# adaLN's later vectors in a pool of their own, half of them beside V, and S1 of h inside the retention

## The chip, the cores and the metric

The kernel runs on one core of a Trainium2 chip. The metric is the time of one execution in microseconds of the device. Before the change it is 1793.54 us, the median of three runs (1792.5 to 1797.46).

## The reference, cut to what matters

One decoder layer on x of 1024 tokens by 1024 channels, all float32. The vector c gives six vectors of 1024 by one matrix, `w_ada`:

```python
mod = jnp.dot(jax.nn.silu(c), w_ada) + b_ada
shift1, scale1, gate1, shift2, scale2, gate2 = split(mod, 6)
h = _rmsnorm(x, norm1_w) * (1.0 + scale1) + shift1
proj = jnp.dot(h, w_in)      # q, k, v of attention, the indexer's iq, ik, iw, retention's q, k, v and gate, two gates
att = _dsa_attention(...)    # each query keeps the 256 keys with the highest indexer score
ret = _retention(...)        # chunks of 128 tokens, four heads, a state carried from chunk to chunk
y_r = jnp.dot(silu(gr) * _head_groupnorm(ret, gn_w), w_ret_proj)
merged = sigmoid(ga) * (att @ w_attn_proj) + sigmoid(gb) * y_r
x = x + gate1 * (merged @ w_out)
h2 = _rmsnorm(x, norm2_w) * (1.0 + scale2) + shift2
x = x + gate2 * ((silu(h2 @ w_ffn_gate) * (h2 @ w_ffn_up)) @ w_ffn_down)
out = _rmsnorm(x, final_norm_w)
```

Only shift1 and scale1 are needed to form h. gate1 is needed at the output projection, and shift2, scale2 and gate2 later still.

## The kernel before, in words

**Arithmetic.** A float32 product is made of three matmuls on rounded parts: each operand is kept as hi (rounded) and lo (the rest), and hi*hi, hi*lo and lo*hi are added up in PSUM. ScalarE (ACT) makes hi by a copy, and GpSimd (POOL) or VectorE (DVE) makes lo by a subtraction. A full block is 128 by 512.

**Stages, in order of the code.** (1) The start: x is normalised, shift1 and scale1 are summed on DVE from `w_ada` (`wa`, `acc`, lines 275 to 294), h^T is made (`hT_hi`, `hT_lo`), and six blocks of the gate projection's first half are multiplied. (2) The indexer's projections. (3) V of attention, with the indexer's scores between its matmuls (lines 491 to 507; `units` and `turns_after` fix how they alternate). (4) Retention, two heads at a time: `for hp in range(2)` from line 606. Each pass has a loop over eight token tiles that makes q and k and rotates them on POOL (lines 610 to 634), and one over the chunks (lines 679 to 692). (5) Six blocks of the gate projection's second half (lines 899 to 905). (6) The other projections, each by seven products of half-sized blocks (M1 to M7, Strassen's scheme, lines 712 to 815, 880 to 992). M1, M2 and M4 multiply blocks of h itself; M5, M6, M3 and M7 multiply four combinations of h's blocks, S1, S2, S4 and S3, in that order. (7) The retention's own projection, attention, the output projection, the FFN.

**The four combinations.** Lines 906 to 916: `add_up` adds the parts on DVE into four `sums` tiles, and `split_sum` makes hi on ACT and lo on DVE. S2 goes on from S1's sums and S4 from S2's, in place; S3 is formed anew and lies where a block of h was. S1, S2 and S4 (16 KB of each partition) are in a pool `sp`, which lies at the addresses of the tables and of the retention's pool `retp`, so each tile waits for what it overlaps there.

**adaLN's other vectors.** `mod_work` (lines 518 to 545) is a generator of 32 steps in four groups of eight: for m = 2, 5, 3, 4 (gate1, gate2, shift2, scale2) and eight rows k of 128, it loads 512 KB of `w_ada` (`mw`, three buffers, two loads ahead) and adds them, scaled by silu(c), into `macc` on DVE (lines 536 and 538). There is one `macc`. A group ends with two matmuls and two additions on DVE into PSUM's sums (`mod_gate`), or eight transposes and two reductions (`mod_cols`). One step is called per token tile in both loops of both retention passes.

**What sets the order.** The tile framework plans every engine's order by a simulation: whenever an engine is free it takes, of the instructions that are ready, the one with the lowest priority number, which is the position in the code. An instruction from further down may therefore come early. `tc.cur_priority += LATE` moves a part back by 20000 positions without any wait. On the chip each engine, and the queue of SyncE (SP) that issues all DMAs, keeps the planned order.

**The selection.** `select_all` (line 440) finds the 256th largest score of each row bit by bit: 31 rounds of six counts over the scores (line 454, DVE), at LATE. It fills DVE from the end of the scores on. `turns_after(paused[0], split)` holds the round of bit 8 behind the last split of S3, and line 1028 that of bit 3 behind the last block of the retention's gated output.

Of the kernel before, what the change touches and what calls it, by code (L numbers as in the profile page):

```python
# [8 lines left out]
F32 = mybir.dt.float32  # L9
# [10 lines left out]
P = 128  # L20
# [23 lines left out]
def tile_hybrid_layer(ctx: ExitStack, tc: tile.TileContext, x, c, w_ada, b_ada, norm1_w, w_in,  # L44
# [159 lines left out]
    def ps_mm():  # L204
        return psx.tile([P, H], F32, name="mm", tag="mm", bufs=3)
# [228 lines left out]
    def all_scores():  # L434
        for b in range(2, NT):
            yield from score_units(b)
        select_all()
# [49 lines left out]
        tc.cur_priority -= LATE  # L487

    units = []
    sgen = all_scores()
    slots = [rows_slot([(w_in, C_VA, H)], k) for k in range(KT)]
    for t in range(NT):
        ps = ps_mm()
        for k in range(KT):
            n = 5 * (KT * t + k) // 4 - 8
            while len(units) <= n and next(sgen, LATE) is not LATE:
                pass
            mm = mm_tok(ps, hT.lhs(t), slots, ks=(k,))  # L500
            if n >= 0:
                turns_after(mm, units[min(n, len(units) - 1)])
        st = projp.tile([P, H], F32, name="vst", bufs=2)
        nc.scalar.activation(st, ps, AF.Copy)
        nc.sync.dma_start(out=v_d[:, t], in_=st)
    for _ in sgen:
        pass
    st_i.close()
    st_p.close()
    st_w.close()  # L510


    st_r = ctx.enter_context(ExitStack())
    retp = pool("retp", side="left", stack=st_r)
    ones = retp.tile([P, P], F32, name="ones")
    nc.vector.memset(ones, 1.0)

    def mod_work():

        steps = [(m, k) for m in (2, 5, 3, 4) for k in range(KT)]  # L520
        mw = {}

        def load(n):
            if n < len(steps):
                m, k = steps[n]
                mw[n] = retp.tile([P, D], F32, name="mw", bufs=3)
                nc.sync.dma_start(out=mw[n], in_=w_ada[k * P:(k + 1) * P, m * D:(m + 1) * D])

        load(0)
        load(1)  # L530
        for n, (m, k) in enumerate(steps):
            load(n + 2)
            sc = silu_c[:, k:k + 1]
            if k == 0:
                acc = retp.tile([P, D], F32, name="macc", bufs=1)
# [27 lines left out]
    def mod_gate(m, i, acc):  # L563
        for hf in range(2):
            cs = slice(hf * H, (hf + 1) * H)
            g = retp.tile([P, H], F32, name="gateb", bufs=1)
# [5 lines left out]
            nc.sync.dma_start(out=gate_d[i][:, cs], in_=g)  # L572


    def ret_scale_col(kind, h):
# [10 lines left out]
    def add_up(out, terms):  # L586

        first = True
        for name, k, sign in terms:
            for part in [out] if name is None else [f32(x[:, k, :]) for x in side[name]]:  # L590
# [6 lines left out]
                    nc.vector.tensor_tensor(out, part, acc, op=ALU.subtract)  # L597
                acc, s0 = out, 1

    def split_sum(to, k, src):  # L600
        hi, lo = (x[:, k, :] for x in side[to])
        nc.scalar.activation(hi, src, AF.Copy)
        return nc.vector.tensor_sub(lo, src, f32(hi))

    mgen = mod_work()
    for hp in range(2):
        slots = [rows_slot([(w_in, C_QR + 256 * hp, 256), (w_in, C_KR + 256 * hp, 256)], k) for k in range(KT)]
        qkT = [big_tile(i, [P, 2, 4, P], F32, "qkT") for i in range(4)]
# [1 line left out]
        for t in range(NT):  # L610
            ps = ps_mm()
            mm_tok(ps, hT.lhs(t), slots)
            qk = retp.tile([P, 4, 2, HD], F32, name="qk", bufs=2)
            for i in range(4):
                nc.scalar.activation(qk[:, i], ps[:, i * P:(i + 1) * P].rearrange("p (a b) -> p a b", a=2),  # L615
                                     AF.Copy, scale=ret_scale_col(i // 2, 2 * hp + i % 2))
            ra = big_tile(6, [P, 4, 2, HD], F32, "rra")
            rb = big_tile(7, [P, 4, 2, HD], F32, "rrb")
            rq = retp.tile([P, 2, 2, HD], F32, name="rq", bufs=2)
            cs = cosr[:, t, :].unsqueeze(1).to_broadcast([P, 8, HD])  # L620
            sn = sinr[:, t, :].unsqueeze(1).to_broadcast([P, 4, HD])
# [12 lines left out]
            next(mgen, None)  # L634
        slots = [rows_slot([(w_in, C_VR + 2 * DV * hp, 2 * DV)], k) for k in range(KT)]
        r = [None, None]
        vs, inns = {}, {}
# [41 lines left out]
        for t in range(NT + 1):  # L679
            if t < NT:  # L680
                ps = ps_mm()
                mm_tok(ps, hT.lhs(t), slots)
                vs[t] = retp.tile([P, 2 * DV], F32, name="vs", bufs=3)
                nc.scalar.activation(vs[t], ps, AF.Copy)
                for e in range(2):
                    inner(t, e)
            if t:
                for e in range(2):
                    r[e] = chunk(t - 1, e, r[e])
            next(mgen, None)  # L690
            if t == 0:
                next(mgen, None)
    for _ in mgen:
        pass
    st_r.close()
    st_t.close()

# [195 lines left out]


    kept = [big_tile(4 + i, [P, 2, H], F32, "kept") for i in range(2)]
    sums = [big_tile(6 + i, [P, 2, H], F32, "sums") for i in range(2)]
    sums = [t[:, i, :] for t in sums for i in range(2)]
# [8 lines left out]
    st_s = ctx.enter_context(ExitStack())  # L906
    sp = pool("sp", side="right", stack=st_s)
    for name in ("S1", "S2", "S4"):
        t = sp.tile([P, 2, 4, H], R, name=name, tag=name)
        side[name] = t[:, 0], t[:, 1]  # L910
# [57 lines left out]
    def behind(i):  # L968
        n, m = 2 + (i - 14) // 7, seq[i][1]
        if 14 <= i < n_mid:  # L970
            if m == "M1":
                flow[n + 1].open()
                flow[n].next = flow[n + 1]
            if n in (8, 9) and m == "M1":
                rope[n - 8] = rope_load(n - 8)
            if n in (9, 10) and m == "M5":
                rope_store(n - 9, *rope[n - 9])
        if i == n_mid:
            flow[-1].open()
        k = i - n_mid - 4  # L980
        if k == -1:
            gT.alloc(0)
        if 0 <= k < KT:
            make_g(k, 0, *g_load(k, 0, *(f32(x) for x in ring_pair())))
            if k in (1, 3):
                stage = sp.tile([P, 8, H], F32, name="stage", tag=f"S{(k + 1) // 2}")
# [699 lines left out]
```

## Time and profile before

| | |
|---|---|
| median of three runs | 1793.54 us |
| profiled execution | 1796.41 us, of which the span from first to last instruction is 1794.6 us |
| granted clock of TensorE, mean | 0.987 of full speed |
| TensorE busy | 1703.6 us (95%) |
| DVE busy | 1211.1 us (67%) |
| POOL busy | 891.7 us (50%) |
| DMA | 266.49 MB, 148 GB/s over the span |

PE is TensorE; a row of a timeline gives start, duration, engine, line, operation, what is written from what, its shape, and in brackets the idle time before it with what ended it. PE's ends are modelled, and 512 columns follow each other every 0.23 us although one is shown as 0.39 us. The granted clock is a share of full speed (1.00 is 2.4 GHz).

### The profile page before, as it was taken

The page shows a single profiled execution, that of the slowest core. Times are in us where ns is not written, and L with a number is a line of the kernel's source. Part 1 is how long each engine was busy: PE and PEld are TensorE (multiplying, and loading weights), DVE is VectorE, ACT ScalarE, POOL GpSimd, SP SyncE. Part 2 cuts the span into 40 slices and gives each one's busy share as a digit, 9 for nine tenths or more (in the row PEclk, how much of TensorE's full clock was granted, in tenths as well). Part 3 has the DMA queues.
Part 4 walks back from the last instruction along what each step waited for, and adds up shares of the span by engine and source line. Part 5 has one row for each costly group of instructions (what it writes and reads, how often), then busy time and mean ns, then how long its engine had stood idle before and what let it go on. Part 6 is the DMA issues. An engine that isn't in the chain of part 4 may idle for free. (4 is left out here: it accounts for less than half of the span.)

```text
span 1794.6 us, 24639 instructions
## 1 busy us (share of the span) xinstructions
PE 1703.6 (95%) x8266; PEld 1399.4 (78%) x8266; DVE 1211.1 (67%) x2093; ACT 747.4 (42%) x1466; POOL 891.7 (50%) x883
## 2 busy tenths in 40 slices
PE   5898989999979999999999999999989999999998
PEld 4797867878758888788777888777778887888887
DVE  7627599999699445459876656876665454476565
ACT  3525532431445344430477246733323333354444
POOL 4571284682565489530246640045444444566574
PEclk9999999999989999999999999999999999999999
DMA  8521245243423356775852740266753332387663
GB/s 278 178 74 42 83 123 185 89 138 95 126 80 116 105 152 195 248 212 159 190 128 69 251 162 1 68 232 235 237 190 106 101 111 89 111 274 227 186 181 113
DMA packets 182655, 266.49 MB, mean 148 GB/s; under 512 B 13872, under 2 KB 111616, under 8 KB 180096
## 3 DMA queue, kind: packets, MB, share of 16 engines
q1 hardware_dynamic: 182528, 264.91, 47.4%
q8 instruction: 65, 1.06, 0.3%
q14 instruction: 62, 0.51, 0.1%
HBM read 195.39 MB, written 69.47 MB: 148 GB/s over the span
## 5 line engine op out<-in xcount | busy, mean ns | idle before, releaser
L80 POOL TENSOR_TENSOR wlo<-wraw,whi 128x512 fp32r<-128x512 f32 (+2 forms) x116 | 144.2, 1253 | 103.6 <-ACT whi L77 96.4
L454 DVE TENSOR_SCALAR_CACHE_REDUCE eq<-score,cand 128x384 uint8<-128x384 f32 (+2 forms) x192 | 180.8, 942 | 4.3
L709 POOL TENSOR_TENSOR flo<-tmp,fhi 128x512 fp32r<-128x512 f32 x79 | 105.1, 1331 | 156.8 <-ACT fhi L708 130.5
L120 PE MATMUL mm<-whi,hT_hi 128*128 128x512 f32 (+1 forms) x432 | 163.3, 381 | 2.4 <-ACT qk L615 1.8
L122 PE MATMUL mm<-wlo,hT_hi 128*128 128x512 f32 (+1 forms) x432 | 163.7, 380 | 0.0
L123 PE MATMUL mm<-whi,hT_lo 128*128 128x512 f32 (+1 forms) x432 | 163.4, 379 | 0.0
L785 PE MATMUL ya<-hc,fhi 128*128 128x512 f32 x344 | 136.1, 396 | 12.1 <-DVE c L768 8.6
L1534 DVE TENSOR_TENSOR dslot<-draw,dslot 128x512 fp32r<-128x512 f32 x88 | 90.4, 1053 | 72.4 <-ACT dslot L1533 66.2
L787 PE MATMUL ya<-hc,fhi 128*128 128x512 f32 x344 | 135.0, 392 | 0.0
L789 PE MATMUL ya<-hc,flo 128*128 128x512 f32 x344 | 133.6, 393 | 0.0
L1533 ACT ACTIVATE dslot<-draw 128x512 fp32r<-128x512 f32 x154 | 90.1, 626 | 97.7 <-PE ya L1552 36.6
L1534 POOL TENSOR_TENSOR dslot<-draw,dslot 128x512 fp32r<-128x512 f32 x66 | 96.9, 1478 | 62.7 <-ACT dslot L1533 58.5
L709 POOL TENSOR_TENSOR flo<-raws,fhi 128x512 fp32r<-128x512 f32 x60 | 83.2, 1387 | 87.8 <-ACT fhi L708 62.8
L77 ACT ACTIVATE whi<-wraw 128x512 fp32r<-128x512 f32 (+2 forms) x116 | 66.8, 589 | 123.2 <-DMA wraw<-in_w_in_dram 59.0
L789 PE MATMUL yb<-hc,flo 128*128 128x512 f32 x256 | 100.1, 391 | 4.0 <-POOL flo L709 4.0
L785 PE MATMUL yb<-hc,fhi 128*128 128x512 f32 x256 | 100.4, 392 | 0.2
L787 PE MATMUL yb<-hc,fhi 128*128 128x512 f32 x256 | 99.7, 389 | 0.0
L708 ACT ACTIVATE fhi<-tmp 128x512 fp32r<-128x512 f32 x84 | 53.0, 630 | 111.4 <-PE ya L787 61.2
L709 POOL TENSOR_TENSOR wlo<-wraw,whi 128x512 fp32r<-128x512 f32 x52 | 80.2, 1552 | 30.9 <-ACT whi L708 24.9
L120 PEld LDWEIGHTS mm<-whi,hT_hi 128*128 128x128 f32 x432 | 82.4, 191 | 14.7 <-ACT qk L615 2.2
L1086 POOL TENSOR_SCALAR sx<-sx,mx 128x128 f32<-128x128 f32 (+7 forms) x64 | 47.4, 746 | 92.5 <-DVE mx L1085 69.7
L123 PEld LDWEIGHTS mm<-whi,hT_lo 128*128 128x128 f32 x432 | 82.9, 192 | 13.0
(403 smaller groups left out, 4918.2 us busy)
## 6 DMA issues: line engine op xcount, KB each, us to landing
draw<-act_d SPq DMA_DIRECT2D x77, 256.0 KB
mw<-in_w_ada_dram SPq DMA_DIRECT2D x32, 512.0 KB
act_d<-c SPq DMA_DIRECT2D x64, 256.0 KB
raw<-in_w_in_dram SPq DMA_DIRECT2D x26, 512.0 KB
raws<-in_w_ffn_gate_dram SPq DMA_DIRECT2D x24, 512.0 KB
raws<-in_w_ffn_up_dram SPq DMA_DIRECT2D x24, 512.0 KB
dw<-in_w_ffn_down_dram SPq DMA_DIRECT2D x22, 512.0 KB
dw_d<-dw SPq DMA_DIRECT2D x11, 1024.0 KB
```

Of the source, the lines that this page charges most:

```text
L77: ins = nc.scalar.activation(hi[:, :n], raw[:, :n], AF.Copy)
L80: nc.gpsimd.tensor_sub(lo[:, :n], raw[:, :n], f32(hi[:, :n]))
L120: ins = nc.tensor.matmul(ps, lhsT=ahi, rhs=whi[:, :n], start=(i == 0), stop=False)
L122: nc.tensor.matmul(ps, lhsT=ahi, rhs=wlo[:, :n], start=False, stop=False)
L123: nc.tensor.matmul(ps, lhsT=alo, rhs=whi[:, :n], start=False, stop=(i == last))
L454: ins = [nc.vector.tensor_scalar(eq[:, :sc.shape[1]], sc, thr[j], None, op0=op, op1=ALU.add, accum_out=cnt[:, j:j + 1]) for j, sc in enume ...
L709: (eng or nc.gpsimd).tensor_sub(lo, src, f32(hi))
L785: mm = nc.tensor.matmul(ps, lhsT=whi[:, k, :], rhs=hhi[:, k, :], start=own and k == 0, stop=False, skip_group_check=True)
L787: nc.tensor.matmul(ps, lhsT=whi[:, k, :], rhs=hlo[:, k, :], start=False, stop=False, skip_group_check=True)
L789: nc.tensor.matmul(ps, lhsT=wlo[:, k, :], rhs=hhi[:, k, :], start=False, stop=k == 3, skip_group_check=True)
L1533: nc.scalar.activation(slot[:, 0], raw, AF.Copy)
L1534: lo_eng.tensor_sub(slot[:, 1], raw, f32(slot[:, 0]))
```

## The change

Three edits. First, `mod_work` moves ahead of V's loop with a pool of its own, `modp`, on the right side of SBUF, where nothing lay from the start to the end of the first retention pass; `mw` has two buffers instead of three and one load ahead instead of two. V's loop calls two steps per token tile, at priorities moved back by LATE // 10, which is 2000 positions: 16 calls, the eight steps of m = 2, its end, and seven steps of m = 5. The first retention pass calls the others, and what is left is run out at its end. Second, the second pass calls none; at chunk 2 it allocates the `sums` and S1, which now lies in a pool `sp1` where `modp` was, and at chunks 3 to 6 it forms S1's sums, splits them, and goes on to S2's sums. Third, the stage before M1 only splits S2 and forms S4 and S3 as before, with S2 and S4 in `sp`.

```diff
+    st_m = ctx.enter_context(ExitStack())
+    modp = pool("modp", side="right", stack=st_m)
+    ones = modp.tile([P, P], F32, name="ones")
+    nc.vector.memset(ones, 1.0)
+    def mod_work():
...
-                mw[n] = retp.tile([P, D], F32, name="mw", bufs=3)
+                mw[n] = modp.tile([P, D], F32, name="mw", bufs=2)
...
-        load(0)
-        load(1)
-        for n, (m, k) in enumerate(steps):
-            load(n + 2)
+        load(0)
+        for n, (m, k) in enumerate(steps):
+            load(n + 1)
...
+    def mod_step():
+        tc.cur_priority += LATE // 10
+        next(mgen, None)
+        tc.cur_priority -= LATE // 10
...
                 turns_after(mm, units[min(n, len(units) - 1)])
+        for _ in range(2):
+            mod_step()
         st = projp.tile([P, H], F32, name="vst", bufs=2)
...
+    def alloc_side(pl, name):
+        x = pl.tile([P, 2, 4, H], R, name=name, tag=name)
+        side[name] = x[:, 0], x[:, 1]
...
             nc.scalar.activation(qkT[t // 2][:, t % 2].rearrange("p h t -> p (h t)"), tp, AF.Copy)
-            next(mgen, None)
+            if hp == 0:
+                next(mgen, None)
...
-            next(mgen, None)
-            if t == 0:
-                next(mgen, None)
-    for _ in mgen:
-        pass
+            if hp == 0:
+                next(mgen, None)
+            elif t == 2:
+                sums = [big_tile(6 + i, [P, 2, H], F32, "sums") for i in range(2)]
+                sums = [x[:, i, :] for x in sums for i in range(2)]
+                alloc_side(sp1, "S1")
+            elif 3 <= t < 7:
+                k = t - 3
+                add_up(sums[k], [("h12", k, 1), ("h22", k, 1)])
+                split_sum("S1", k, sums[k])
+                add_up(sums[k], [(None, k, 1), ("h11", k, -1)])
+        if hp == 0:
+            for _ in mgen:
+                pass
+            st_m.close()
+            st_s = ctx.enter_context(ExitStack())
+            sp1 = pool("sp1", side="right", stack=st_s)
...
-    for to, terms in (("S1", [("h12", 1), ("h22", 1)]), ("S2", [(None, 1), ("h11", -1)]),
-                      ("S4", [(None, -1), ("h21", 1)]), ("S3", [("h11", 1), ("h12", -1)])):
+    for to, terms in (("S2", []), ("S4", [(None, -1), ("h21", 1)]), ("S3", [("h11", 1), ("h12", -1)])):
         for k in range(4):
-            add_up(sums[k], [(n, k, sign) for n, sign in terms])
+            if terms:
+                add_up(sums[k], [(n, k, sign) for n, sign in terms])
             split = split_sum(to, k, sums[k])
```

## Rows read from the trace of the kernel before

**Rows 1.** The page's head and its busy time by engine.
```profile
span 1794.6 us, 24639 instructions
PE 1703.6 (95%) x8266; PEld 1399.4 (78%) x8266; DVE 1211.1 (67%) x2093; ACT 747.4 (42%) x1466; POOL 891.7 (50%) x883
```

**Rows 2.** Stretches: length, busy time (count) of PE, PEld, DVE, ACT, POOL; PE's clock, DMA.
```profile
13.00:66.00 53.00, 38.29 (x169) 29.75 (x170) 50.29 (x94) 17.97 (x33) 30.25 (x26) 0.97 0.75 236
66.00:130.00 64.00, 62.95 (x438) 59.56 (x438) 19.94 (x44) 22.20 (x41) 40.16 (x90) 1.00 0.39 110
130.00:230.00 100.00, 94.38 (x451) 78.73 (x449) 65.40 (x106) 56.37 (x112) 23.41 (x25) 0.98 0.21 63
228.00:300.00 72.00, 63.71 (x277) 50.23 (x276) 69.23 (x114) 21.60 (x55) 54.88 (x64) 0.95 0.59 186
495.00:550.00 55.00, 44.14 (x174) 34.53 (x173) 52.55 (x62) 25.06 (x45) 31.50 (x18) 0.91 0.29 86
```

**Rows 3.** PE's order of time: the start of M1, and the first and last wait behind it.
```profile
504.36 0.50 PE L785 MATMUL mm<-hT_hi,whi 128*128 128x512 f32 x1 [0.15 <-ACT spare L904]
515.88 0.50 PE L785 MATMUL mm<-S,whi 128*128 128x512 f32 x1 [3.07 <-ACT kept L765]
533.41 0.80 PE L787 MATMUL lg<-S,whi 128*128 128x512 f32 x1 [1.84 <-DVE S L603]
```

**Rows 4.** Stretches, `sums` alone: busy time of DVE and ACT, then POOL, clock, DMA.
```profile
405.00:430.00 25.00, 7.48 (x12) 0.00 (x0) 0.00 (x0) 1.00 0.13 32
495.00:550.00 55.00, 39.88 (x45) 10.83 (x18) 0.00 (x0) 0.91 0.29 86
```

**Rows 5.** DVE's order of time: splits of the combinations, and the selection's next count.
```profile
497.91 3.48 DVE L603 TENSOR_TENSOR S<-sums,S 128x512 fp32r<-128x512 f32 x2
511.84 0.68 DVE L603 TENSOR_TENSOR S<-sums,S 128x512 fp32r<-128x512 f32 x1
548.63 0.60 DVE L454 TENSOR_SCALAR_CACHE_REDUCE eq<-score,cand 128x384 uint8<-128x384 f32 x1
```

**Rows 6.** A stretch between retention and the combinations.
```profile
480.00:490.00 10.00, 10.00 (x46) 8.28 (x45) 3.39 (x13) 3.10 (x7) 3.59 (x11) 1.00 0.24 81
```

**Rows 7.** `macc`: its additions over the whole span (min/median/max ns, first and last start).
```profile
L538 DVE SCALAR_TENSOR_TENSOR macc<-mw,colT,macc x28: 1268/1318/2166, 236.4 to 447.2; 128x1024 f32<-128x1024 f32 x28
```

**Rows 8.** The first group of steps: DVE, POOL and PE in order of time.
```profile
236.36 1.98 DVE L538 SCALAR_TENSOR_TENSOR macc<-mw,colT,macc 128x1024 f32<-128x1024 f32 x1
239.59 1.43 POOL L627 TENSOR_TENSOR rq<-rra,rrb 128x128 f32<-128x128 f32 x1
259.02 0.47 POOL L627 TENSOR_TENSOR kk<-rra,rrb 128x128 f32<-128x128 f32 x1
241.90 0.33 PE L631 MATMUL tr<-ident,rq 128*128 128x128 f32 x1 [1.73 <-POOL rq L628]
250.55 0.33 PE L632 MATMUL tr<-ident,kk 128*128 128x128 f32 x1 [1.06 <-POOL kk L628]
```

**Rows 9.** The second and third group: PE's waits, and the stretches that hold them.
```profile
294.73 0.49 PE L643 MATMUL tr<-qkT 128*128 128x128 f32 x2 [1.99 <-DVE inn L645]
372.41 0.33 PE L631 MATMUL tr<-ident,rq 128*128 128x128 f32 x1 [2.74 <-POOL rq L628]
250.00:260.00 10.00, 9.45 (x38) 7.67 (x39) 9.75 (x17) 2.33 (x6) 9.84 (x15) 0.83 0.48 153
290.00:300.00 10.00, 8.01 (x31) 6.24 (x30) 9.89 (x22) 0.38 (x1) 0.00 (x0) 0.83 0.95 332
370.00:380.00 10.00, 6.71 (x24) 5.20 (x25) 9.75 (x17) 1.74 (x5) 9.71 (x14) 0.83 0.52 178
```

**Rows 10.** SP: the load of gate1, whose line stands behind attention in the code.
```profile
L1214 SPq DMA_DIRECT2D gate<-gate_d x1: 430/430/430, 291.8 to 291.8; - x1
```

**Rows 11.** DVE in the start: lines of the last tiles of x between `acc`'s.
```profile
50.37 0.75 DVE L235 TENSOR_SCALAR x_t<-x_t,rstd 128x1024 f32<-128x1024 f32 x1
51.38 0.48 DVE L287 SCALAR_TENSOR_TENSOR acc<-wa,colT,acc 128x256 f32<-128x256 f32 x1
```

More of the change, by code (lines that the diff above doesn't have):

```diff
@@ L487, in select_all @@
         tc.cur_priority -= LATE
[L491 to L498, printed above, removed]
-                pass
[L500 to L515, printed above, removed]
+    st_m = ctx.enter_context(ExitStack())
+    modp = pool("modp", side="right", stack=st_m)
+    ones = modp.tile([P, P], F32, name="ones")
     nc.vector.memset(ones, 1.0)
@@ L525, in load @@
                 m, k = steps[n]
-                mw[n] = retp.tile([P, D], F32, name="mw", bufs=3)
+                mw[n] = modp.tile([P, D], F32, name="mw", bufs=2)
                 nc.sync.dma_start(out=mw[n], in_=w_ada[k * P:(k + 1) * P, m * D:(m + 1) * D])
         load(0)
-        load(1)
         for n, (m, k) in enumerate(steps):
-            load(n + 2)
+            load(n + 1)
             sc = silu_c[:, k:k + 1]
             if k == 0:
-                acc = retp.tile([P, D], F32, name="macc", bufs=1)
+                acc = modp.tile([P, D], F32, name="macc", bufs=1)
                 nc.vector.tensor_scalar(acc, mw[n], sc, None, op0=ALU.mult)
@@ L565, in mod_gate @@
             cs = slice(hf * H, (hf + 1) * H)
-            g = retp.tile([P, H], F32, name="gateb", bufs=1)
+            g = modp.tile([P, H], F32, name="gateb", bufs=1)
             nc.sync.dma_start(out=g, in_=b_ada[m * D + hf * H:m * D + (hf + 1) * H]
@@ L572, in mod_gate @@
             nc.sync.dma_start(out=gate_d[i][:, cs], in_=g)
+    mgen = mod_work()
+    def mod_step():
+        tc.cur_priority += LATE // 10
+        next(mgen, None)
+        tc.cur_priority -= LATE // 10
+    units = []
+    sgen = all_scores()
+    slots = [rows_slot([(w_in, C_VA, H)], k) for k in range(KT)]
+    for t in range(NT):
+        ps = ps_mm()
+        for k in range(KT):
+            n = 5 * (KT * t + k) // 4 - 8
+            while len(units) <= n and next(sgen, LATE) is not LATE:
+                pass
+            mm = mm_tok(ps, hT.lhs(t), slots, ks=(k,))
+            if n >= 0:
+                turns_after(mm, units[min(n, len(units) - 1)])
+        for _ in range(2):
+            mod_step()
+        st = projp.tile([P, H], F32, name="vst", bufs=2)
+        nc.scalar.activation(st, ps, AF.Copy)
+        nc.sync.dma_start(out=v_d[:, t], in_=st)
+    for _ in sgen:
+        pass
+    st_i.close()
+    st_p.close()
+    st_w.close()
+    st_r = ctx.enter_context(ExitStack())
+    retp = pool("retp", side="left", stack=st_r)
     def ret_scale_col(kind, h):
@@ L603, in split_sum @@
         return nc.vector.tensor_sub(lo, src, f32(hi))
-    mgen = mod_work()
     for hp in range(2):
@@ L689, in tile_hybrid_layer @@
                     r[e] = chunk(t - 1, e, r[e])
-            next(mgen, None)
-            if t == 0:
+            if hp == 0:
                 next(mgen, None)
-    for _ in mgen:
-        pass
+            elif t == 2:
[9 more added lines that the diff above has]
+            for _ in mgen:
+                pass
+            st_m.close()
+            st_s = ctx.enter_context(ExitStack())
+            sp1 = pool("sp1", side="right", stack=st_s)
     st_r.close()
@@ L895, in tile_hybrid_layer @@
     kept = [big_tile(4 + i, [P, 2, H], F32, "kept") for i in range(2)]
-    sums = [big_tile(6 + i, [P, 2, H], F32, "sums") for i in range(2)]
-    sums = [t[:, i, :] for t in sums for i in range(2)]
     quads = [t[:, i, :] for t in kept for i in range(2)] + [spare] + sums
@@ L905, in tile_hybrid_layer @@
         nc.sync.dma_start(out=sgb_d[nt][:, H:], in_=to)
-    st_s = ctx.enter_context(ExitStack())
     sp = pool("sp", side="right", stack=st_s)
-    for name in ("S1", "S2", "S4"):
-        t = sp.tile([P, 2, 4, H], R, name=name, tag=name)
-        side[name] = t[:, 0], t[:, 1]
+    for name in ("S2", "S4"):
+        alloc_side(sp, name)
     side["S3"] = side["h12"]
-    for to, terms in (("S1", [("h12", 1), ("h22", 1)]), ("S2", [(None, 1), ("h11", -1)]),
-                      ("S4", [(None, -1), ("h21", 1)]), ("S3", [("h11", 1), ("h12", -1)])):
+    for to, terms in (("S2", []), ("S4", [(None, -1), ("h21", 1)]), ("S3", [("h11", 1), ("h12", -1)])):
         for k in range(4):
-            add_up(sums[k], [(n, k, sign) for n, sign in terms])
+            if terms:
+                add_up(sums[k], [(n, k, sign) for n, sign in terms])
             split = split_sum(to, k, sums[k])
@@ L985, in behind @@
             if k in (1, 3):
-                stage = sp.tile([P, 8, H], F32, name="stage", tag=f"S{(k + 1) // 2}")
+                stage = (sp1, sp)[k // 2].tile([P, 8, H], F32, name="stage", tag=f"S{(k + 1) // 2}")
                 for i in range(4):
```

## The prediction

> **What bounds the kernel now.** I read the page's head, then the stretches, then each engine's order of time where PE falls behind. Over the span PE is busy 95%, DVE 67%, POOL 50% [rows 1]: the kernel is bound by TensorE, and only places where PE is short can be won or lost. The profiled execution took 1796.41 us, 1.8 us more than its span and 2.9 us above the median of the runs shown (1793.54); I work the sum out against 1796.41 and carry it over to the median.
>
> Three places touch the change. The start, 13 to 66: PE 38.3 of 53 us, DVE 50.3 of 53 [rows 2], so DVE sets the pace. Retention, 228 to 300: PE 63.7 of 72, DVE 69.2 of 72, POOL 54.9 [rows 2]. The combinations, 495 to 550: PE 44.1 of 55 at a clock of 0.91, DVE 52.6 of 55 [rows 2]. Between them, 66 to 130 and 130 to 230, PE is nearly full and DVE has 44 and 35 us free [rows 2]. The chain of waits says little here, since nearly all of it is PE behind PE.
>
> **Part A: the combinations.** What can be won at most: PE is idle for 55 - 44.14 = 10.9 us, and a clock of 0.91 (a mixture of 1.2 and 2.4 GHz) costs (1 - 0.91) x 55 = 5.0 us, together 15.8 us. M1 starts at 504.36; behind it PE waits four times for a combination, first at 515.88 and last at 533.41 [rows 3]. In that stretch DVE spends 39.9 us on 45 operations of `sums`, 0.89 us each [rows 4], since some take 0.68 and some 1.74 (two in 3.48) [rows 5]. S1's twelve sums were done early already, at 405 to 430 [rows 4]; what goes from here is S1's four splits and S2's eight additions, 12 x 0.89 = 10.6 us. The last split now ends at 548.6, where the selection goes on [rows 5]; then at about 538. A free PE would need S3 for M7 after four pairs of products: 24 matmuls each, at 0.23 us, 5.5 us a pair, so from 504.4 + 22 = 526 to 532. So with the same beginning DVE is still some 6 us late at M7, and the gain is 10.6. If the splits of S2 (four, some 3.6 us) move into the time before, where DVE is busy 3.4 of 10 us [rows 6], nearly all 15.8 comes back. But S2 lies, as before, where the retention's own tiles lay, and may start no earlier; then its four splits are first in the queue instead of S1's. Bounds 4 (S2 stays late) and 15.8; I take 11, the DVE time itself.
>
> The moved work (12 sums, 4 splits, 8 additions) lands in the second pass, where DVE loses two groups of eight steps, 8 x 1.32 = 10.6 us each [rows 7]; the 12 additions were there before. I price it at nothing: the selection, which fills DVE, gives way. Without that cover each operation would cost the chain of chunks up to its 0.89 us, 12 us for the 12 new ones on DVE. The selection's round of bit 8 waits for the last split and is released earlier than before, not later.
>
> **Part B: the retention without half of the steps.** Each of the four groups is eight operations on DVE, 1.27 to 2.17 us each [rows 7]. The first group falls in the rotation on POOL: `macc` takes 1.98 us there instead of 1.27, and POOL's `rq` 1.43 where the same shape takes 0.47 undisturbed [rows 8]. PE waits three times for POOL, 1.73, 1.72 (the row between, of the same kind) and 1.06, the first and last shown [rows 8], and its clock falls to 0.83 for 10 us [rows 9]: 4.5 + 1.7 = 6.2 us. The second group delays the mask's product `inn`, PE waits 1.99, and the clock is 0.83 again [rows 9]: 3.7. The third group, in the second pass's rotation, costs PE 10 - 6.71 = 3.3 and 1.7 of clock [rows 9]: 5.0. The fourth shows no wait. Together 14.9 us. After the change the second pass has no step, so the 5.0 go. Of the first pass's two groups, m = 3 and m = 4 stand there now; but their place differs: a group starts when the one `macc` is free, and that needs the matmuls at the end of the group before, which PE takes by priority. m = 2 and m = 5 are done before, so m = 3 may well stand in the rotation as m = 2 did. I take 3.7 + 5.0 and no gain at the first group: 8.7, say 9. Bounds 0 and 14.9.
>
> The Trainium skill ("SBUF — State Buffer", Who interferes with whom) says that a DVE instruction with two inputs in SBUF and a GpSimd instruction that reads SBUF shut each other out for the whole instruction. The trace agrees: POOL's 1.43 us is 0.96 over its 0.47. By that rule the additions of S1 in the second pass, which read two SBUF inputs, would give back some of these 9 us wherever POOL works; at one wait of 0.96 for each of the 12 new operations that would be 11.5 us of POOL's time.
>
> **Part C: how early the steps come.** The code calls 16 steps beside V, but a call's place is only a priority. gate1's load stands behind attention and was issued at 291.8, as soon as its source had been written [rows 10], and the lines for the last tiles of x, which stand behind all of `acc`'s code, were planned between `acc`'s operations [rows 11]. `modp` overlaps nothing earlier, so the first two loads are ready at time 0 and the steps of m = 2 as soon as silu(c) is there; the 2000 positions put them behind whatever is ready, not behind the start. I therefore expect the eight steps of m = 2 in the start, and no more: their end needs a PSUM bank of the kind that the start's six sums hold to its end, and m = 5 needs the same `macc`. In the start DVE is full [rows 2], so eight steps at 1.27 to 2.17 us add 10 to 17 us to DVE's chain, and 4 MB join a stretch whose DMA engines are busy 0.75 [rows 2]. Some steps may fall in DVE's last 2.7 free us or behind the chain. Nothing leaves the start, so there is no gain in it. Bounds 0 and 17; I take 11, near the undisturbed row (8 x 1.32 = 10.6). SP's queue carries these loads ahead of loads for the start and for the indexer's weights, and a load that waits for a buffer holds those behind it; that is in the upper bound.
>
> **Part D: the steps in the indexer's stage and in V.** m = 5 falls there: 8 x 1.32 = 10.6 us of DVE and its ends, against 44 and 35 us free [rows 2]. Behind a delayed score stand ACT's next relu and PE's next score. Where DVE's free time is in pieces below 1.3 us, each step can push a score back. POOL is busy only 23.4 of 100 us in V [rows 2], so there is little to collide with. Bounds 0 and 8 (half of each step and a bit of DMA wait); I take 2. The matmuls and transposes at the ends of the groups move and cost PE the same.
>
> **The sum.** -11 (A) - 9 (B) + 11 (C) + 2 (D) = -7 us: 1796.4 - 7 = 1789.4 as a profiled execution; from the median 1793.5 - 7 = 1786.5, rounded down to 1786 because A's upper half is likelier than its lower one.
>
> **The rivals.**
> 1. The steps do stand beside V. Then C is 0 and D carries all 16 steps, 21 us of DVE against 34.6 us free in V [rows 2], say 4. -11 - 9 + 4 = -16: 1777. For it: V is where they are called, and POOL is quiet there. Against it: rows 10 and 11.
> 2. Slower: the start takes the steps and stalls on their DMA. A step planned between two `acc` operations holds DVE until its 512 KB have landed, and the 0.5 MB loads stand in SP's queue ahead of `wa`. At 236 GB/s, the rate of that stretch [rows 2], 4 MB take 18 us; DVE's chain and the wait add to 23, with A at 5 and B at 5: +13 with D, less a few: about +11, 1804. It decides as soon as the start loses more than A and B return, about 20 us. For it: DVE and DMA are both near full. Against it: DVE is busy 50.3 of 53 us there [rows 2], so it hardly waits for loads now and they have some lead.
> 3. The change trades places: S2's splits wait for the retention's tiles as S1's did, so A is 5; the first pass keeps two costly groups and B is 5; C is 8 and D 2. Sum 0: 1793.5. For it: the row of S2's first splits, 497.9, stands right behind the retention's end, and S2 overlaps it still.
>
> **How the numbers follow.** The forecast has 0.36, rival 1 0.28, rival 2 0.18, rival 3 0.18. What a measurement of this kernel can tell from no change is 0.3%, 5.4 us: 1788.2 to 1798.9 is the same. The forecast lies below 1788.2 in two thirds of its cases (0.25), rival 1 in all but a few (0.27), rival 3 in a fifth (0.04): faster 0.56. Same: 0.10 of the forecast, 0.01 of rival 1, 0.11 of rival 3, 0.02 of rival 2: 0.24. Slower: 0.20. The forecast's own range is 1780 to 1792; for 8 in 10 it must reach to rival 1's middle and towards rival 2: 1771 to 1802.
>
> **What would show it.** A: the waits of PE behind M1 shrink from four to one at most, at M7; the clock of 495 to 550, shifted, is 1.00 or near; `sums` has 33 operations there instead of 45. B: no PE wait for `rq` in the second pass's rotation. C: `macc` written before 66 us, eight times, and DVE's chain for shift1 and scale1 ending 10 us or more later. D: `macc` between 76 and 230. The prediction is wrong if no `macc` stands in the start, or if it does and the start is no longer; and if PE waits as often for S2 and S4 as before.

## The result, and the profile after

The change makes the kernel slower, by 0.7%: 1803.97 us, the median of 20 runs (1795.92 to 1813.25), against 1792.65 for the kernel before, run beside it (20 runs). The ratio is 1.0069, 95% interval [1.0054, 1.0083], +11 to +12 us. The forecast was 1786 us, range 1771 to 1802.

The profiled run of the change took 1798.3 us, 5.7 below its median; that of before took 1796.4, 3.8 above the median of the 20. So the pair differs by 1.9 us only, and I go by two profiles of the changed kernel, this one and a second (e1 below, 1806.2 us, near the median). Where the time goes, by landmarks in the order of time:

| us | before | after, first | after, second |
|---|---|---|---|
| start: first gate copy (`gstage`) | 76.4 | 88.0 | 88.7 |
| first copy of the retention's q and k (`qk`) | 229.8 | 247.5 | 249.1 |
| first product of M1 | 501.3 | 505.1 | 514.6 |
| attention's first score (`lga`) | 864.8 | 865.2 | 874.6 |
| end of the execution | 1796.4 | 1798.3 | 1806.2 |

Read as differences between neighbours, first profile minus before: start +11.6, indexer and V +6.1, retention and gate blocks -13.9, M1 to attention -3.4, the rest +1.5; together +1.9. The second: +12.3, +7.0, **-6.0**, -3.5, 0.0; together +9.8. The two profiles of one kernel differ in the retention.

The stretches of the first profile, as in [rows 2]:
```profile
13.00:66.00 53.00, 38.01 (x153) 30.82 (x154) 51.37 (x93) 16.11 (x28) 25.02 (x22) 0.87 0.88 294
66.00:130.00 64.00, 58.87 (x382) 54.93 (x381) 28.95 (x49) 21.60 (x40) 37.42 (x77) 0.92 0.47 138
130.00:230.00 100.00, 92.58 (x456) 75.77 (x456) 68.56 (x109) 50.33 (x100) 29.28 (x39) 0.98 0.36 107
228.00:300.00 72.00, 69.58 (x315) 55.64 (x314) 59.77 (x94) 29.09 (x69) 56.65 (x67) 1.00 0.42 121
495.00:550.00 55.00, 49.15 (x203) 39.32 (x202) 50.13 (x68) 24.25 (x45) 36.54 (x20) 0.94 0.25 79
```
The start moves 294 GB/s instead of 236 and its clock falls from 0.97 to 0.87; 66 to 130, where PE was nearly full, loses 4 us of PE and clock 0.92; the retention's first stretch is nearly full; at the combinations part of the gap is left.

DVE in the start (the first and last two rows of the eight `macc`, and the last `acc`):
```profile
24.61 0.74 DVE L512 TENSOR_SCALAR macc<-mw,colT 128x1024 f32<-128x1024 f32 x1
27.01 2.03 DVE L514 SCALAR_TENSOR_TENSOR macc<-mw,colT,macc 128x1024 f32<-128x1024 f32 x1
...
69.49 1.27 DVE L514 SCALAR_TENSOR_TENSOR macc<-mw,colT,macc 128x1024 f32<-128x1024 f32 x1
73.00 1.27 DVE L514 SCALAR_TENSOR_TENSOR macc<-mw,colT,macc 128x1024 f32<-128x1024 f32 x1
...
74.20 0.99 DVE L287 SCALAR_TENSOR_TENSOR acc<-wa,colT,acc 128x256 f32<-128x256 f32 x2
```
All eight steps of m = 2 stand in the start, and `acc` ends at 75 instead of 65. ACT's last split of the start's own weights is as late, and waits for a load (before: 64.17, after no wait):
```profile
75.02 0.52 ACT L77 ACTIVATE whi<-wraw 128x384 fp32r<-128x384 f32 x1 [3.73 <-DMA wraw<-in_w_in_dram]
```

Before the change, the two waits of PE that stand between those of [rows 3]:
```profile
521.40 0.79 PE L787 MATMUL mm<-S,whi 128*128 128x512 f32 x1 [2.92 <-DVE S L603]
530.05 0.50 PE L787 MATMUL lg<-S,whi 128*128 128x512 f32 x1 [2.88 <-DVE S L603]
```
M1 and what follows after it, PE; then ACT; then DVE's last splits of S3; then `sums` alone against [rows 4]:
```profile
505.14 0.39 PE L812 MATMUL mm<-hT_hi,whi 128*128 128x512 f32 x1
...
516.89 0.50 PE L812 MATMUL mm<-S,whi 128*128 128x512 f32 x1 [0.70 <-ACT kept L792]
...
530.50 0.79 PE L812 MATMUL lg<-S,whi 128*128 128x512 f32 x1 [5.14 <-ACT kept L792]
```
```profile
527.01 0.63 ACT L617 ACTIVATE hT_hi<-sums 128x512 fp32r<-128x512 f32 x1 [8.17 <-DVE sums L606]
...
529.88 0.58 ACT L792 ACTIVATE kept<-lg 128x512 f32<-128x512 f32 x1
```
```profile
531.72 1.88 DVE L618 TENSOR_TENSOR hT_lo<-sums,hT_hi 128x512 fp32r<-128x512 f32 x3
```
```profile
495.00:550.00 55.00, 28.88 (x33) 8.52 (x14) 0.00 (x0) 0.94 0.25 79
```
Four waits (10.7 us together) became two (5.8), in front of M6 and of M3's second product, and the 33 `sums` forecast are there. DVE's last split ends at 533.6 instead of 548.6, earlier than the 538 forecast. But ACT stands 8.17 us in front of S3's first split, with the copy that PE needs behind it. And from 550 to 600, where PE had no idle time before, it now waits 2.9 us in three places, the first of them shown; the second profile has the same three. Before, after, and the wait:
```profile
550.00:600.00 50.00, 50.00 (x222) 41.29 (x221) 42.05 (x86) 19.92 (x36) 20.34 (x15) 1.00 0.33 108
```
```profile
550.00:600.00 50.00, 47.11 (x204) 38.00 (x205) 35.85 (x67) 18.67 (x34) 19.55 (x14) 1.00 0.37 119
```
```profile
570.92 0.50 PE L812 MATMUL mm<-hT_hi,whi 128*128 128x512 f32 x1 [1.74 <-ACT kept L792]
```

**The missing 8 us.** The second profile, at the retention's end: DVE, POOL, PE.
```profile
411.07 8.80 DVE L459 TENSOR_SCALAR rej<-cnt 128x6 int32<-128x6 f32 x1
419.90 0.17 DVE L474 SCALAR_TENSOR_TENSOR cand<-cand,rej 128x6 int32<-128x6 int32 x1
```
```profile
409.20 2.57 POOL L80 TENSOR_TENSOR wlo<-wraw,whi 128x512 fp32r<-128x512 f32 x2
411.70 1.32 POOL L636 TENSOR_TENSOR rra<-qk,cosr 128x512 f32<-128x512 f32 x1
...
419.33 0.50 POOL L642 TENSOR_TENSOR kk<-rra,rrb 128x128 f32<-128x128 f32 x1
```
```profile
438.17 0.79 PE L658 MATMUL tr<-qkT 128*128 128x128 f32 x2 [6.61 <-DVE inn L660]
```
`rej`, six columns of the selection, takes 0.17 us undisturbed. Here it takes 8.80, and ends at 419.87, when POOL's string of instructions ends (419.83). DVE is that much late, and from 431.6 to 438.17 PE waits for `inn`. In the first profile the same `rej`, at the same place in the same string, found its turn at the end of the POOL instruction that was running (`wlo`, 410.16):
```profile
409.47 0.72 DVE L459 TENSOR_SCALAR rej<-cnt 128x6 int32<-128x6 f32 x1
```
The stretch of 400 to 495 therefore differs; first profile, then second:
```profile
400.00:495.00 95.00, 94.74 (x440) 78.51 (x439) 80.06 (x193) 36.04 (x74) 47.90 (x81) 1.00 0.32 91
```
```profile
400.00:495.00 95.00, 88.39 (x405) 73.78 (x404) 85.56 (x189) 34.05 (x70) 45.53 (x73) 0.96 0.28 80
```
Both profiles also have a shorter one, in the first half: a `rej` of 3.8 us (at 297 and 299), and 1.8 us of PE waiting for `inn` behind it.

### The profile page after: what moved, and what is told of

It is laid out like the page before. It is cut to its first block, busy times and chain, and to the rows that moved or that the text cites. A ratio compares the mean times of both kernels' runs of the same rounds, so it can differ in the third digit from the quotient of the medians.

```text
span 1796.5 us, 24643 instructions
## 1 busy us (share of the span) xinstructions
PE 1707.1 (95%) x8266; PEld 1399.4 (78%) x8266; DVE 1211.2 (67%) x2093; ACT 746.6 (42%) x1466; POOL 891.9 (50%) x883
```

## The experiments

The ratios are to the kernel before, run beside each. PE's waits and `rej`'s durations are from the one profiled run of each.

**e1, the changed kernel again.**

> The changed kernel again, unedited, for a second profile and times of the same chip as the three below. Theory (time is lost in the start to the eight steps of m=2, and won back only in part): 11 us above the kernel before (ratio 1.005 to 1.008), last store of the start near 88 us against 77, S1 and the retention give 15 and 3 us back in the profile. What the first profile leaves open: by its stretches the change costs 2 us, by the medians 11. If the start's time hangs on its transfers, this profile, when its time is a typical one, has the missing 9 us before 90 us; the rival has them after 1136 us, in stretches that the change does not touch.

Measured: 1803.57 us, ratio 1.0051 [1.0030, 1.0072]. The missing time is neither in the start nor behind 1136 us: both places that I had named were wrong; it is the stall shown above.

**e2, no step in the start; e3, no loads; e4, thin steps.**
```diff
 e2 (last_store is the start's last store of the gate)
-                nc.sync.dma_start(out=mw[n], in_=...)
+                ld = nc.sync.dma_start(out=mw[n], in_=...)
+                if n < 2:
+                    turns_after(ld, last_store[0])
 e3
+                if 0 < n < KT:
+                    mw[n] = mw[0]        # mw[0] is filled by a memset, not loaded
+                    return
 e4
+                w = 16 if m == 2 else D
-                nc.vector.scalar_tensor_tensor(acc, mw[n], sc, acc, ...)
+                nc.vector.scalar_tensor_tensor(acc[:, :w], mw[n][:, :w], sc, acc[:, :w], ...)
```


> The first two loads of the steps wait in program order for the start's last store, so that no step of m=2 stands in the start. Theory: the start is back at 77 us, the steps go to the indexer and V, the retention and S1 stay as in the changed kernel: 12 to 18 us below the changed kernel, 1 to 7 us below the kernel before (ratio to before 0.996 to 0.999). Rival (VectorE's time only moves: the steps cost V or the indexer what they cost the start): within 4 us of the changed kernel, ratio 1.005 to 1.009. Third (the loss lies outside the start): less than 4 us below the changed kernel, with the start's last store back at 77 us all the same.

> The eight steps of m=2 read one constant tile in place of their rows, so the 4 MB of loads are gone and VectorE's work stays (gate1 is not computed rightly). Theory (VectorE is what the steps cost the start, about 11 us): the start ends near 87 us as in the changed kernel, and the time stays within 4 us of it. Rival (the loads cost: they share the DMA engines with the start's own and VectorE stands in order behind them): the start ends near 78 us, and the time falls by 8 to 14 us.

> The steps 2 to 8 of m=2 work on 16 columns of their 1024, with their loads whole (gate1 is not computed rightly): VectorE is freed of about 9 us, the transfers stay. Theory (VectorE): the start ends near 79 us, the time falls by 8 to 10 us. Rival (the loads): the start ends near 87 us, and the time stays within 3 us of the changed kernel.

Measured: e2 1796.77, ratio 1.0014 [1.0000, 1.0028]; e3 1800.87, 1.0041 [1.0024, 1.0058]; e4 1802.19, 1.0050 [1.0031, 1.0069]. The start's gate copies, for e2, e3, e4 (first and last start of the first three):
```profile
L259 ACT ACTIVATE gstage<-mm x3: 592/597/602, 76.1 to 77.4; 128x512 f32<-128x512 f32 x3
```
```profile
L257 ACT ACTIVATE gstage<-mm x3: 591/600/602, 82.6 to 83.9; 128x512 f32<-128x512 f32 x3
```
```profile
L257 ACT ACTIVATE gstage<-mm x3: 592/597/603, 88.1 to 89.4; 128x512 f32<-128x512 f32 x3
```
My theory that the eight steps' DVE time is the start's price does not hold. Without loads the start is still 6.2 us late; without most of the DVE work it is as late as ever, 11.7 us. In e4 `acc` ends at 67, but the start's weights come late all the same:
```profile
73.89 1.26 ACT L77 ACTIVATE whi<-wraw 128x384 fp32r<-128x384 f32 x3 [2.83 <-DMA wraw<-in_w_in_dram]
```
So the loads are enough for the whole delay by themselves, as e4's rival said, and with the loads gone about half of it is left, between e3's theory and its rival. These are no exact prices: in e3 the eight steps, which wait for no load, stand from 7 to 23 us, four of them before 13, and two loads of m = 5 are still issued in the start. e2 wins the start back whole and 7 us of the total, less than its theory and more than its rivals; the last copy of V is at 233.7 there, against 234.7 in the changed kernel and 216.3 before: nearly all of the start's gain is gone again by V's end. (Between e2's profile and the first of the changed kernel, both without the long stall, there are 4.4 us; whether e2 also meets the stall less often is not shown.)

**e5 to e7, `rej` from two inputs.** A tile `pow2` of 128 bytes a partition is made first:
```diff
-            nc.vector.tensor_scalar(rej, cnt, float(TOPK), float(value), op0=ALU.is_lt, op1=ALU.mult)
+            nc.vector.scalar_tensor_tensor(rej, cnt, float(TOPK), pow2[:, bit:bit + 1].to_broadcast([P, n]),
+                                           op0=ALU.is_lt, op1=ALU.mult)
```


> The kernel before, with the selection's rej (6 columns) formed by an operation with two inputs in SBUF (cnt, and a column of powers of two) in place of one input and a constant. In the traces so far that small operation took 0.17 us mostly, but 3.8, 6.3, 8.8 or 11.8 us where GpSimd ran a string of instructions without a gap, and always to the end of that string; cand, which has two inputs, never took over 1.3 us. Theory (rej stands out GpSimd's strings): no rej over 1.4 us is left, and the kernel before, which has about 27 us of slack in VectorE's order there, gains 0 to 3 us (ratio 0.998 to 1.000). Rival (VectorE is held by any small operation there): cand or rej still takes 4 us or more.

> The same edit in the changed kernel. Theory (the part of its loss that its first profile did not show is rej's 8.8 us at 411, after which S1's adds keep inn back and TensorE waits 6.6 us): no such wait, 5 to 8 us below the changed kernel, 1 to 5 us above the kernel before (ratio 1.001 to 1.003), and its own runs closer together. Rival (the missing time hangs on the start's loads): within 3 us of the changed kernel, ratio 1.004 to 1.007.

> The same edit together with the hold that keeps the steps of m=2 out of the start. If the two losses are apart from each other, the sum of both: 10 to 14 us below the changed kernel, 0 to 5 us below the kernel before (ratio 0.997 to 1.000). If the hold had gained only because rej met GpSimd otherwise, no more than the edit alone: ratio 1.001 to 1.003.

Measured: 1807.1, ratio 1.0072 [1.0058, 1.0087]; 1816.35, 1.0128 [1.0111, 1.0146]; 1814.79, 1.0114 [1.0095, 1.0133]. All three theories fell; e5's rival, that `rej` still takes 4 us or more, held. `rej` with two inputs stands out POOL's strings as well, 5.87 us in e5 and 11.86 in e6; that `cand` never did fits its place behind `rej`, when the string is over. And something else was changed: from about 500 to 1500 us the matmuls follow each other more slowly at the same granted clock, 216 of them in 50 us where the kernel before has 222. Before, then e5, with its `rej`:
```profile
600.00:650.00 50.00, 50.00 (x222) 41.43 (x221) 18.07 (x17) 20.26 (x37) 33.25 (x25) 1.00 0.45 133
```
```profile
600.00:650.00 50.00, 50.00 (x216) 40.19 (x216) 16.34 (x16) 19.22 (x34) 33.08 (x24) 1.00 0.44 130
```
```profile
L463 DVE SCALAR_TENSOR_TENSOR rej<-cnt,pow x31: 136/166/5865, 259.0 to 831.7; 128x6 int32<-128x6 f32 x31
```
So these times say nothing on the stall. The slower matmuls stay unexplained; the tile shifts later tiles' addresses, which I did not vary. Between e5 and e6, both with it, the change costs 9 us, as between the two kernels.

**e8, S1 back at M1, the adaLN part kept.** S1 is allocated in `sp` again and its loops stand where the kernel before has them:
```diff
-                alloc_side(sp1, "S1")
...
+    for name in ("S1", "S2", "S4"):
+    for to, terms in (("S1", [("h12", 1), ("h22", 1)]), ("S2", [(None, 1), ("h11", -1)]), ...
+                    turns_after(ins, last_inn[0])      # in add_up
```


> The changed kernel with S1 back where the kernel before has it (its pool, sums and splits behind the retention, its first adds held behind the last inn); the adaLN part stays. Theory: the start ends 11 us late and V 18 us late as in the changed kernel, the second half of the retention has no S1 in VectorE's order, so a long rej finds slack and TensorE does not wait for inn; at M1 the loss is that of the kernel before (idle 9.5 and clock near 0.91 in 495 to 550). The two about cancel: 1800 to 1805 us, ratio 1.003 to 1.006. Rival 1 (S1 in the retention is the gain that the change has): 5 us or more above the changed kernel, ratio over 1.008. Rival 2 (S1 in the retention is what costs): at most 1.002.

Measured: 1806.8, ratio 1.0076 [1.0052, 1.0101], between the theory and rival 1. The trace says more: `rej` takes 8.80 us at 410 and PE waits 6.27 for `inn` although no sum of S1 stands there. So S1's additions, 5.7 us of which stand right in front of `inn` in the second profile, are not needed for the wait: in e8 the selection's rounds alone stand ahead of `inn` in DVE's order. From the first `qk` to M1 e8 takes 264.5 us and the second profile 265.5, both with the stall, so the moved work itself costs about 1 us there. And M1 to attention takes 363.9 us (513.1 to 877.0) as before the change (363.5): S1's move is worth the 3.4 us there.

**e9 and e11, gaps for `rej`.** A real wait on POOL for a DVE instruction; the orders are nearly those of the changed kernel (in e11 some 3% of DVE's rows stand elsewhere). GAPS names pass, tile and the rotation's instruction (0 `rra`, 1 and 2 `rrb`, 3 the first `rq`) and the `rej` that it waits for; e9 has the last entry alone:
```diff
+GAPS = {(0, 6, 3): 3, (0, 7, 1): 4, (1, 7, 0): 16}
+            for (p, u, i), n in GAPS.items():
+                if (p, u) == (hp, t):
+                    tc.add_manual_dep(rot[i].ins, rejs[n].ins.name, SYNC, reason="a gap for rej")
```


> The changed kernel with one wait added: GpSimd's first rotation product of the retention's last query and key tile (second half, t = 7) waits for the selection's 17th rej. Every engine's order stays. In three of the profiles that rej took 8.8 us, to the end of GpSimd's last string of instructions at 420, and TensorE then waited 6.3 to 6.6 us for inn; in three others it found a gap at an instruction's end and took 0.7 to 0.9 us. Theory (a typical run of the changed kernel has the long one): with the gap that rej takes under 1 us in every run, there is no wait of 6 us at 430, and the median falls by 4 to 7 us, to a ratio of 1.001 to 1.003. Rival (the long rej goes with a slow run by chance, the time hangs on something else): ratio 1.005 to 1.007.

> The changed kernel with three waits on GpSimd in place of one: the first rq of the rotation's tile t = 6 (first half) waits for the 4th rej, the first rrb of t = 7 for the 5th, and as before the first product of t = 7 (second half) for the 17th. In the run with one gap the 4th rej took 11.8 us at 289 and TensorE waited 8.1 us for inn at 315; the 17th had become short. Theory (a typical run of the changed kernel has one of these two long stalls): rej stays under 2.5 us everywhere, no wait of TensorE over 4 us between 240 and 495, the median 4 to 8 us below the changed kernel, ratio 1.000 to 1.003. Rival (the stall only moves on, to a wait or to GpSimd, since VectorE is behind anyway): ratio 1.004 to 1.007.

Measured: e9 1802.49, ratio 1.0050 [1.0031, 1.0069]; e11 1794.18, 1.0009 [0.9993, 1.0024]. e9's time is that of its rival: the 17th `rej` is short, but the 4th was caught by the string of the first half:
```profile
289.22 11.84 DVE L462 TENSOR_SCALAR rej<-cnt 128x6 int32<-128x6 f32 x1
```
```profile
315.64 1.22 PE L663 MATMUL tr<-qkT 128*128 128x128 f32 x4 [8.13 <-DVE inn L665]
```
With gaps at both strings (e11) no `rej` is over 1.42 us, PE has no wait for `inn`, and the 9 us are gone:
```profile
L463 DVE TENSOR_SCALAR rej<-cnt x32: 147/356/1417, 267.0 to 826.7; 128x6 int32<-128x6 f32 x32
```
```profile
400.00:495.00 95.00, 94.80 (x441) 78.69 (x440) 79.16 (x191) 36.12 (x74) 48.14 (x82) 1.00 0.33 92
```
That is the cause of the loss that the first profile lacked, and other profiles bear it out: from the first `qk` to M1 it takes 257 to 258 us in four without a long stall (the first, e2, e3, e14), 264 to 266 in three with one (e1, e8, e9), and 270.6 in e4, which has both, with 8.13 and 6.63 us of PE behind them:
```profile
287.15 11.83 DVE L459 TENSOR_SCALAR rej<-cnt 128x6 int32<-128x6 f32 x1
...
412.40 8.82 DVE L459 TENSOR_SCALAR rej<-cnt 128x6 int32<-128x6 f32 x1
```
The 27 times of the changed kernel fit, but show less: five stand apart, from 1811 to 1814, where both stalls would put them; the other 22 lie from 1794 to 1807 with no gap over 1.6 us. Which of them had a stall is known for the two profiled ones alone. e11's 11 lie from 1788.9 to 1800.2.

**e10, e12 and e13, the steps in the retention's first half.** `modp` opens behind V, the first two loads stand behind V's sixth store, two steps per place; e12 adds one gap, e13 holds S3's splits on ACT behind the copy of M5's second product:
```diff
 e10
+                if n < 2:
+                    turns_after(ld, vstores[5])
             if hp == 0:
                 next(mgen, None)
+                next(mgen, None)
 e12
+GAPS = {(1, 7, 2): 15}
 e13 (and, alone on the changed kernel, e14)
+    for to, k, i in split_acts:
+        if to == "S3":
+            turns_after(i, flow[1].m5)
```


> The steps' pool is opened behind V instead of ahead of it, and the first two loads wait in program order for V's sixth store: all 32 steps and both gates stand between V's end and the middle of the retention, two in each place where the changed kernel has one; S1 stays in the retention's second half. Theory (what the steps cost is VectorE's time in the start, 11 us, and beside V, 6 us, where TensorE waits for it): start and V end as in the kernel before, at 77 and near 217 us, the retention's first half is a few us longer, the gain of its second half and of M1 stays: 10 to 17 us below the changed kernel, ratio 0.994 to 1.000. Rival (VectorE has no room anywhere before 440 us, so the steps cost the same in the retention's first half): the retention ends at 495 us or later as in the changed kernel's typical run, ratio 1.004 to 1.007.

> The steps held back until V's end, as in e10, and one gap: GpSimd's second rrb of the last tile (second half) waits for the 16th rej, which took 6.3 us at 399 there, before TensorE waited 5.5 us for inn at 423. Theory: that wait goes, 3 to 6 us below e10, ratio 0.996 to 0.999. Rival (stalls move on): ratio 0.999 to 1.001.

> e12, and S3's four first copies on ScalarE (hT_hi from sums) stand behind the copy of the second stream's M5 product. In the changed kernel and in e10 ScalarE stood 8 us in front of them, with that copy behind it in order, and TensorE waited 4.6 to 5.1 us. Theory (ScalarE's order is what is late next at M1 once S1 is out of it): that wait shrinks below 1 us, 3 to 6 us below e12, ratio 0.993 to 0.997. Rival (VectorE's sums of S3 are late anyway): the wait appears at M7 or at hT_lo, within 2 us of e12.

> The changed kernel with that order of ScalarE alone. Theory: 495 to 550 loses 5 us less, the median 3 to 6 us below the changed kernel, ratio 1.001 to 1.004. Rival: within 2 us of it, ratio 1.005 to 1.007.

Measured: e10 1794.3, ratio 0.9996 [0.9980, 1.0013]; e12 1784.6, 0.9960 [0.9945, 0.9975]; e13 1783.45, 0.9953 [0.9936, 0.9971]; e14 1803.14, 1.0058 [1.0041, 1.0076]. In e10 the start ends at 76.1 and V's last copy is at 219.3, so both costs are gone, and the stall (6.26 us at 399, PE 5.48 for `inn`) eats the gain; e12 takes it away, and beats both kernels; both came out at the edge of their theories' ranges. (e12's and e13's profiled runs are the slowest of theirs, 7.8 and 4.8 us over the medians, without a long `rej`; what makes them slow is not known.) For e13 and e14 the rivals held: the order of ACT is not what is late next at M1: in e14 and e13 the wait is 5.9 us instead of 5.1 and 4.65, and stands further on, in front of the first product of the tile that holds S3 (`hT_hi`). DVE ends S3's sums at 530.96; PE is let go by the copy `spare`, which stands behind S3's four splits on ACT. e14, ACT and PE:
```profile
526.77 0.63 ACT L619 ACTIVATE hT_hi<-sums 128x512 fp32r<-128x512 f32 x1 [8.27 <-DVE sums L606]
```
```profile
532.67 0.80 PE L814 MATMUL mm<-hT_hi,whi 128*128 128x512 f32 x1 [5.94 <-ACT spare L794]
```

**e15 and e16, the gaps in the kernel before and with e2's hold.** GAPS is {(1, 7, 2): 17} in e15, and e11's in e16.

> The kernel before with one gap: GpSimd's second rrb of the last tile (second half) waits for the 18th rej, which took 6.3 us at 403 in its profile. Theory (the kernel before has slack there, TensorE did not wait for inn after it): the stall goes and the time stays, 0 to 2 us, ratio 0.999 to 1.001. Rival (the stall costs the kernel before too, some time later): 3 to 6 us below it, ratio 0.996 to 0.998.

> The changed kernel with the hold of e2 (no step of m = 2 in the start) and the three gaps of e11: both runs without the long stall, so that what is left between them is what the eight steps cost in the start. e11 was at a ratio of 1.001. Theory (11 us in the start, some 4 of them given back since the steps then stand in the indexer): 5 to 9 us below e11, ratio 0.996 to 0.998. Rival (all of it moves on to the indexer and V): within 2 us of e11.

Measured: e15 1790.71, ratio 0.9989 [0.9972, 1.0006]; e16 1790.77, 0.9984 [0.9968, 0.9999]. In e15 the long `rej` only shrank, from 6.28 to 4.32, and the gain of 2 us can't be told from none: what the stall costs the kernel before stays open between 0 and 5 us. e16 against e11 is 0.0025 of ratio, 4.5 us, give or take 4 by the two intervals, and just short of its theory's 5 to 9. e16 still has a `rej` of 4.61 us, with 0.57 of PE behind it; with no longer one in the way, the 4.5 us are what the steps of m = 2 cost by standing in the start instead of the indexer (in the profiles 11.8 at the start's end, 5.0 at M1).

## Why the prediction was wrong

**C was right in size, in part by luck.** Forecast +11, measured +11.6, and the eight steps are in the start. But I priced DVE's time and left the loads to rival 2; by e4 the loads cost the whole 11.7 alone, and by e3 the steps without them 6.2. And of what the start loses, some 4.5 us are left at the end (e16 against e11).

**D was too small:** +2 forecast, +6.1 to +7.0 measured, within its bound of 8, and all of it in V: 88.3 us from V's first copy to its last, 81.1 before. DVE's free time in V is in pieces between scores, as the part says; but DVE also waited 2.5 us for `mw`, 0.9 for the bias of the gate, and the held scores reached PE (waits of 0.25, 0.43, 0.43 and 1.27 us from 201 to 216). These are 2.4 us; where the rest went is not shown.

**A was the mis-sized term:** -11 forecast, bounds -4 to -15.8, measured -3.4, outside. The step that failed: "A free PE would need S3 for M7 ... the gain is 10.6". The 12 operations did go, and DVE's end came 15.0 us earlier (533.6, before 548.6). But PE does not follow DVE's end one to one: it waits for a chain, S2, S4, S3, whose last sums still run against POOL. In e14 four of S3's additions take 1.77 us each where others take 0.68. So in place of four waits behind M1 (10.7 us) PE has 0.70 in front of M6 and 5.14 in front of M3's second product, and 2.9 us more from 550 to 600, which I had not thought of. The part also read M1's start wrongly: 504.36 is the second of M1's two products, the first starts at 501.3 (the table above), so a free PE needs S3 at 523 to 529, and DVE's forecast end at 538 was 9 us late for it, not 6.

**B failed in its cover.** -9 forecast, bounds 0 to -14.9; -13.9 in the first profile, -6.0 in the typical one. The wait at 372 went as forecast. That for `inn` at 295 did not; it has another cause now, the `rej` of 3.79 at 297:
```profile
309.43 0.71 PE L658 MATMUL tr<-qkT 128*128 128x128 f32 x4 [1.83 <-DVE inn L660]
```
What the forecast had not counted came instead: the waits for `rq` and `kk` in the first rotation fell from 4.5 to 2.4 us, and the clock from the first `qk` to M1 is 1.00, before 0.98. The sentence that failed is "the selection, which fills DVE, gives way" (it stands in part A): it cannot. The order is fixed when the kernel is planned, and its rounds stand ahead of `inn`; each of them has a `rej` that can stand to the end of POOL's string. The moved work itself was rightly priced near nothing (about 1 us, by e8); what the sum lacked is the stall. Before the change a `rej` of 6.28 us at 403 was followed by no wait of PE for `inn` until 465 (0.83). In the changed kernel, which enters the retention 18 us later and does it in 14 us less, the same stall reaches PE as 6 to 8 us. e11 shows that such stalls are the difference between the two profiles.

The Trainium skill ("SBUF — State Buffer", Who interferes with whom), which I drew on for S1's additions, says that VectorE and GpSimd lock each other out of a shared pair of ports for the whole instruction, and counts a `tensor_scalar` among those that can take it. The trace agrees on who is locked out, but shows more: DVE stayed locked out through ten POOL instructions in a row (8.80 us; each takes 0.50 to 1.33), not one. So the rule was at hand, for an instruction that I did not look at; but priced at one POOL instruction, at most 1.33 us, it would not have given the stall.

**The sum.** Forecast -11 - 9 + 11 + 2 = -7. The first profile: -3.4 - 13.9 + 11.6 + 6.1 = +0.4, and 1.5 behind attention. The typical run: -3.5 - 6.0 + 12.3 + 7.0 = +9.8. Of the rivals the second, slower, gave the time (1804): its A and B, -5 and -5, were nearly right; its C of 23 was not, and its sum was wrong: 23 - 5 - 5 with D's 2 is 15, not 13.

## What to carry to other kernels

A part that a planner may take early is not where the code calls it: if it must not stand in a full stage, hold its first load there, and look whether the next stages are any better (e2 gained 7 us, e12, with the steps in the retention's first half and a gap, about 18). One profile of a kernel whose engines meet by chance is one draw: compare its own time with the median, and if they differ by more than the effect, take a second profile before explaining anything. Work that "fills" an in-order engine gives way to nothing; what matters is what is queued behind it.

## What the runs showed of the hardware

- A 6-column DVE instruction, 0.17 us undisturbed, took 3.8, 6.3, 8.8 and 11.8 us beside POOL, each time to the end of a string of POOL instructions without a gap, with one input or two; three POOL instructions made to wait for it (e11) cut the longest to 1.4 us and won 9 us.
- From the same place in the same string it took 0.72 us in one run and 8.80 in another. What decides is not settled.
- With a tile of 128 bytes added among the constants, matmuls of the middle of the kernel followed each other in 231 instead of 225 ns (50 us over 216 and 222) at a granted clock of 1.00, worth some 14 us in e5. Not explained.
